# A planner's prices for TensorE, for whole float32 products and for the port that two engines share, in a two-layer encoder

## The chip, the core and the metric

The kernel runs on one core of one Trainium2 chip. The core has a matrix engine (TensorE, PE in the profile, with a second row PEld for its weight loads), VectorE (DVE), ScalarE (ACT), GpSimd (POOL), and SyncE (SP), which only issues transfers. The metric is the device time of one execution in microseconds; less is better.

## What is computed

The reference is a two-layer streaming encoder over 1024 tokens of 1024 values, in float32. Layer 0 mixes with a gated causal convolution of 31 taps beside a gated linear recurrence, layer 1 with differential attention (two softmax maps per head, eight heads, rotary positions, a mask by chunks of 64). After each mixer and each feed-forward part comes a residual sum and a layer norm:

```python
for layer in range(DEPTH):
    y = conv_lru_mixer(x, ...) if layer % 2 == 0 else diff_attention_mixer(x, ...)
    x = layer_norm(DN_ALPHA * x + y, mix_ln_g[layer], mix_ln_b[layer])
    x = layer_norm(DN_ALPHA * x + (silu(x @ w_gate) * (x @ w_up)) @ w_down, ffn_ln_g[layer], ffn_ln_b[layer])
```

The feed-forward part is 2816 wide.

## The kernel before

**Products.** A float32 product of full accuracy is made of three products in the engine's faster float32 format (fp32r): `three` takes operands that are split into a high part and a rest and issues high by high, high by rest, rest by high. `split` makes the two parts: ScalarE casts the source to the high part, and VectorE subtracts it from the source. This subtraction is the row `xt<-g,xt` or `g<-g,g ... fp32r` of the profile; when its source is in the matrix engine's result memory (PSUM, tile `PS`), it is `xt<-PS,xt`. Nearly all products are 128x128 by 512 columns. Four products alone, those of the mean and the variance in `conv_mean` and `conv_var`, are whole float32 ones of 512 columns; the profile shows each of them as two records `PS<-g,SM`. Transposes go through the matrix engine as well, with float32 operands (`PS<-SM,g 128x128`).

**Stages.** Layer 0's mixer runs first. Its second token half is mixed with the lead of the feed-forward part: `ffn_lead` computes two of the seven products of a Strassen-like scheme for each of the 22 strips of the hidden width, and `operands_b` turns tokens into operands by `x_operand`, which subtracts or adds on VectorE, transposes four blocks on PE and splits the result. `ffn_up` then takes one strip after another, with five products (60 matrix instructions) a strip: GpSimd adds or subtracts weight halves (`w_operand`), ScalarE casts, VectorE subtracts, PE multiplies, VectorE and GpSimd combine. `ffn_down` does seven more products. Layer 1 mixes attention with another stream twice: the first half of the queries with the projections of the later heads, the second half with the lead of the second feed-forward part. In attention, `attn_rms` has two GpSimd powers of one element for every pair of query blocks, 32 pairs in all, and each of the 32 layer norms has one.

**The planner.** Nothing of the order on an engine is left to the text of the program. Each instruction that is emitted is recorded by `Order.note`, with its dependences, a price in nanoseconds from `Order.price` and its engine. `Order.solve` then makes a schedule. Going backward it gives each instruction a due time: the matrix instructions are put in program order one behind the other by their prices, and what feeds them is due before them by its own price and by `lag`; on the other engines the due times are also pushed apart by 0.81 of the price. Going forward it plays the five engines in time: among what is ready, each engine takes the instruction due first, and its price is added to the engine's clock. At the end `apply` fixes the order found on every engine by dependences that cost no semaphore. The planned times go nowhere else: the chip runs the fixed orders at its own pace. The prices of instructions on VectorE, ScalarE and GpSimd, the constants `margin`, `press`, `tail`, `patience` and `switch`, and the emission with its own constant `MM` for mixing two streams are not touched by the change.

Of the kernel before, what the change touches and what calls it, by code (L numbers as in the profile page):

```python
# [10 lines left out]
F32 = mybir.dt.float32  # L11
# [73 lines left out]
class Order:  # L85
# [82 lines left out]
    def note(self, eng, name, ins, a, k):  # L168
        i = len(self.ops)
        deps = {}  # L170
        aps = [x for x in (*a, *k.values()) if hasattr(x, "ap") and hasattr(x, "tensor")]
        out = a[0] if a else k["out"]
        outs = [out] + [k[x] for x in ("accum_out",) if x in k]
        reads = [x for x in aps if not any(x is o for o in outs)]
        for x in reads:
            self.touch(i, deps, x, False)
        for x in outs:
            self.touch(i, deps, x, True)
        op = Op(i, ins, eng, deps)
        op.cost, op.table = self.price(eng, name, out, reads, a, k)  # L180
        op.dma = name == "dma_start"
        op.label = name
        self.ops.append(op)

    def price(self, eng, name, out, reads, a, k):
        n = 1
        for s in out.shape[1:]:
            n *= s
        if name == "dma_start":
            b = 4 * n * out.shape[0]  # L190
            return b / 360.0, None
        if eng == "pe":
            whole = reads[0].dtype == F32
            if name == "transpose":
                return 109.2, None
            if n < 256:
                return (214.0 if whole else 107.0), None
            return (n / 2.4 + 2.5) * (4 if whole else 1), None
        psum = any(x.name.startswith("PS") for x in (out, *reads))
        if eng == "act":  # L200
            f = a[2] if name == "activation" else None
            fn = str(f).split(".")[-1] if f is not None else "Copy"
            src = reads[0] if reads else out
            t = 0.833 * n + (52 if src.name.startswith("PS") else 94)
            if hasattr(k.get("bias"), "ap"):
                t += 50
            if hasattr(k.get("scale"), "ap"):
                t += 93 if not hasattr(k.get("bias"), "ap") else 137
            if "accum_out" in k:
                t += 93  # L210
            return t, SETS.get(fn)
        if eng == "dve":
            if name in ("tensor_reduce", "bn_stats"):
                n = 1
                for s in reads[0].shape[1:]:
                    n *= s
            if name in ("tensor_copy", "memset"):
                return (0.52 if name == "tensor_copy" and not psum else 1.0417) * n + (69 if name == "tensor_copy" else 7), None
            if name == "reciprocal":
                return 6.25 * n + 69, None  # L220
            t = 1.0417 * n + 69
            if name == "tensor_scalar":
                t = 0.75 * n + 70
            elif name == "scalar_tensor_tensor" and hasattr(a[2], "ap"):
                t += 61
            return t, None
        if eng == "pool":
            if n <= 4:
                return 1000.0 if name == "tensor_tensor" else 700.0, None
            return (2.7 * n + 150 if name == "tensor_tensor" else 0.9 * n + 280 if name == "tensor_scalar" else n + 60), None  # L230
        return 50.0, None
# [10 lines left out]
    def solve(self):  # L242
        ops = self.ops
        n = len(ops)
        succ = [[] for _ in range(n)]
        for o in ops:
            for d, raw in o.deps.items():
                succ[d].append((o.i, raw))

        t = 0.0  # L250
        late = [0.0] * n
        for o in ops:
            if o.eng == "pe":
                late[o.i] = t
                t += o.cost
        last = t
        gone = dict.fromkeys(self.ENGINES, 1e12)
        need = [len(x) for x in succ]
        heap = [(-1e12, -o.i) for o in ops if not need[o.i]]
        heapq.heapify(heap)  # L260
        while heap:
            i = -heapq.heappop(heap)[1]
            o = ops[i]
            dur = o.cost + (1100 if o.dma else 0)
            x = min((late[s] - self.lag(o, ops[s], raw) for s, raw in succ[i]), default=last + self.tail) - dur
            if o.eng == "pe":
                x = min(x, late[i])
            elif o.eng != "sp" and not o.dma:
                e = o.eng
                x = min(x, gone[e] - o.cost * self.press)  # L270
                gone[e] = x
            late[i] = x
            for d in o.deps:
                need[d] -= 1
                if not need[d]:
                    heapq.heappush(heap, (-min(late[s] - self.lag(ops[d], ops[s], raw) for s, raw in succ[d]), -d))
        self.late = late

        est = [0.0] * n
        left = [len(o.deps) for o in ops]  # L280
        free = dict.fromkeys(self.ENGINES, 0.0)
        ready = {e: [] for e in self.ENGINES}
        order = {e: [] for e in self.ENGINES}
        for o in ops:
            if not left[o.i]:
                ready[o.eng].append(o.i)
        table = None
        hw = ring = 0.0
        pick = {}
        dirty = set(self.ENGINES)  # L290
        self.start = [0.0] * n
        done = 0
        while done < n:
            for e in dirty:
                r = ready[e]
                if not r:
                    pick[e] = None
                    continue
                t0 = max(free[e], min(est[i] for i in r))
                slack = {"dve": 130, "act": 60, "pool": 60}.get(e, 0)  # L300
                best = None
                for i in r:
                    if est[i] > t0 + slack:
                        continue
                    key = late[i]
                    if est[i] > t0:
                        key += self.patience
                    if e == "act" and ops[i].table and table not in ops[i].table:
                        key += self.switch
                    if best is None or key < best[0]:  # L310
                        best = (key, i)
                pick[e] = (max(t0, est[best[1]]), best[1])
            dirty = set()
            e = min((p for p in pick if pick[p]), key=lambda p: pick[p][0])
            s, i = pick[e]
            o = ops[i]
            ready[e].remove(i)
            order[e].append(i)
            if e == "act" and o.table and table not in o.table:
                table = o.table[0]  # L320
                s += 1283
            self.start[i] = s
            if o.dma:
                if e == "pool":
                    free[e] = s + 900
                    b = free[e] + 2000
                else:
                    free[e] = s + 60
                    hw = max(hw, s + 25) + 450
                    b = hw + 1600  # L330
                ring = max(ring, b) + o.cost
                end = ring
            else:
                end = free[e] = s + o.cost
            dirty.add(e)
            for j, raw in succ[i]:
                est[j] = max(est[j], end + self.lag(o, ops[j], raw))
                left[j] -= 1
                if not left[j]:
                    ready[ops[j].eng].append(j)  # L340
                    dirty.add(ops[j].eng)
            done += 1
        self.total = max(free.values())
        return order
# [18 lines left out]


class Op:
    __slots__ = ("i", "ins", "eng", "deps", "cost", "table", "dma", "label")

    def __init__(self, i, ins, eng, deps):
        self.i, self.ins, self.eng, self.deps = i, ins, eng, deps
# [1588 lines left out]
```

## Time and profile before

| | us |
|---|---|
| median of 3 runs | 2277.43 |
| fastest and slowest run | 2267.81, 2277.70 |
| the profiled execution | 2272.42 |
| its span, first to last instruction | 2270.6 |
| PE busy in the span | 2151.8 (95%) |
| VectorE busy | 1852.9 (82%) |
| ScalarE busy | 1025.0 (45%) |
| GpSimd busy | 980.8 (43%) |

The profile is one execution. Busy time is that of instructions in flight; matrix instructions overlap, so what one of them takes from the engine is read from the distance between starts or from a count in a stretch, not from its own length. The engine's granted clock is a share of its full 2.4 GHz; the mean over the span is 0.979.

### The profile page before, as it was taken

To read this page: it belongs to the slowest core of one execution; us is meant where nothing else is said; L and a number is where in the kernel's file an instruction comes from. 1 tells how busy PE (TensorE), PEld (TensorE's weight loads), DVE (VectorE), ACT (ScalarE), POOL (GpSimd) and SP (SyncE) were. 2 spreads that over 40 slices of the span, in tenths; PEclk is the share of its full clock that TensorE was granted. 3 is DMA by queue.
4 is the path that set the end of the run, shared out by engine and by line. 5 is a ranking of instruction groups with operands and counts; after the bars stand their busy time and mean duration, and the time that the engine had idled before them with its cause. 6 is when DMAs were issued, how large, how long until landed. Compare 5 with 4: busy or idle time off the path is not lost.

```text
span 2270.6 us, 28995 instructions
## 1 busy us (share of the span) xinstructions
PE 2151.8 (95%) x9856; PEld 1769.1 (78%) x9856; DVE 1852.9 (82%) x2747; ACT 1025.0 (45%) x1791; POOL 980.8 (43%) x762
## 2 busy tenths in 40 slices
PE   9999898999999999989999997989989999999997
PEld 7877776778888888868878775877777888888885
DVE  8978799897888698884888867777878887778887
ACT  6485437343333334642455444555634333344362
POOL 1122412177777454221344324222334867755622
PEclk9999999999999999999999998999999999999999
DMA  8446986374454959846556589676737444477776
GB/s 238 94 111 158 264 240 192 116 271 150 149 159 153 317 142 224 224 112 208 160 160 176 150 238 245 187 192 173 199 107 254 167 160 158 161 210 249 177 181 170
DMA packets 173539, 419.74 MB, mean 185 GB/s; under 512 B 18896, under 2 KB 39120, under 8 KB 173392
## 3 DMA queue, kind: packets, MB, share of 16 engines
q1 hardware_dynamic: 145168, 364.47, 50.3%
q0 software_dynamic: 28224, 53.43, 13.9%
q8 instruction: 78, 1.28, 0.2%
q14 instruction: 69, 0.57, 0.1%
HBM read 313.03 MB, written 85.98 MB: 176 GB/s over the span
## 4 chain that ended last, share of the span: by engine, by line
PE 66%; DMA 16%; DVE 9%; issue 4%; ACT 3%; POOL 1%; SPq 1%; DVEq 0%; POOLq 0%; ACTq 0%
PE PS L380 66%; DVE g L380 6%; DMA g<-in_down 5%; DMA g<-in_up 4%; ACT g L380 2%; DMA g<-g 2%; DVE xt L380 2%; DMA z_d<-g 1%; DMA g<-k_d 1%; DVE SM L380 1%; POOL g L380 1%; DMA g<-a_d 1%; DMA g<-in_wout 1%; SPq L380 1%; DMA k_d<-g 1%
## 5 line engine op out<-in xcount | busy, mean ns | idle before, releaser
L380 POOL TENSOR_TENSOR g<-g,g 128x512 f32<-128x512 f32 (+1 forms) x368 | 601.1, 1645 | 518.2 <-DVE g L380 243.9
L380 PE MATMUL PS<-xt 128*128 128x512 f32 x2536 | 668.9, 392 | 15.3 <-ACT xt L380 6.6
L380 PE MATMUL PS<-g,xt 128*128 128x512 f32 (+1 forms) x2800 | 648.8, 379 | 11.9 <-ACT g L380 7.5
L380 PE MATMUL PS<-xt,g 128*128 128x512 f32 x2428 | 612.6, 401 | 37.6 <-ACT g L380 23.5
L380 PEld LDWEIGHTS PS<-g,xt 128*128 128x128 f32 x2800 | 516.2, 190 | 118.4 <-ACT g L380 11.1
L380 PEld LDWEIGHTS PS<-xt,g 128*128 128x128 f32 x2428 | 459.7, 192 | 143.2 <-ACT g L380 28.6
L380 PEld LDWEIGHTS PS<-xt 128*128 128x128 f32 x2536 | 475.9, 189 | 117.0 <-ACT xt L380 8.4
L380 ACT CAST xt<-g 128x512 fp32r<-128x512 f32 x567 | 334.5, 619 | 513.0 <-PE PS L380 330.8
L380 DVE TENSOR_TENSOR xt<-g,xt 128x512 fp32r<-128x512 f32 x567 | 496.9, 901 | 83.0 <-ACT xt L380 78.1
L380 DVE TENSOR_TENSOR g<-g,g 128x512 f32<-128x512 f32 (+2 forms) x442 | 449.5, 1027 | 68.8 <-ACT g L380 57.6
L380 DVE TENSOR_TENSOR g<-PS,g 128x512 f32<-128x512 f32 (+3 forms) x408 | 255.7, 641 | 131.8 <-PE PS L380 102.2
L380 ACT CAST g<-g 128x512 fp32r<-128x512 f32 (+1 forms) x212 | 167.2, 796 | 200.1 <-DVE g L380 67.2
L380 DVE SCALAR_TENSOR_TENSOR g<-g,SM,g 128x512 f32<-128x512 f32 (+20 forms) x301 | 250.2, 865 | 5.9 <-POOL SM L380 3.8
L380 ACT ACTIVATE g<-PS,SM 128x512 f32<-128x512 f32 (+8 forms) x266 | 179.4, 688 | 151.9 <-PE PS L380 91.8
L380 PE MATMUL PS<-xt,xt 128*128 128x512 f32 (+1 forms) x612 | 212.9, 390 | 0.0
L380 PE MATMUL PS<-g,g 128*128 128x512 f32 (+3 forms) x768 | 197.2, 367 | 13.8 <-ACT g L380 7.8
L380 PEld LDWEIGHTS PS<-g,g 128*128 128x128 f32 x768 | 132.6, 190 | 40.0 <-ACT g L380 10.3
L380 POOL DMA_DIRECT2D g<-in_down x88 | 84.4, 1053 | 169.8 <-DMA g<-in_down 161.4
L380 POOL TENSOR_TENSOR SM<-SM 128x1 f32<-128x1 f32 x96 | 85.0, 928 | 149.0 <-DVE SM L380 148.6
L380 POOL DMA_DIRECT2D g<-g x64 | 60.1, 1023 | 192.7 <-ACT g L380 131.8
L380 POOL TENSOR_TENSOR g<-g 128x512 f32<-128x512 f32 x74 | 114.0, 1581 | 63.1 <-DMA g<-in_gate 33.0
L380 PE MATMUL PS<-SM,g 128*128 128x128 f32 (+1 forms) x704 | 111.4, 284 | 29.8 <-DVE g L380 20.4
(49 smaller groups left out, 1200.4 us busy)
## 6 DMA issues: line engine op xcount, KB each, us to landing
g<-in_up SPq DMA_DIRECT2D x88, 512.0 KB, 4.3
g<-in_down SPq DMA_DIRECT2D x176, 256.0 KB, 3.6
z_d<-g SPq DMA_DIRECT2D x44, 512.0 KB, 4.5
g<-in_gate SPq DMA_DIRECT2D x44, 512.0 KB, 4.2
g<-z_d SPq DMA_DIRECT2D x44, 512.0 KB, 4.2
g<-in_down POOLq DMA_DIRECT2D x88, 256.0 KB, 6.7
a_d<-g SPq DMA_DIRECT2D x36, 512.0 KB, 2.9
g<-a_d SPq DMA_DIRECT2D x36, 512.0 KB, 6.7
```

Source lines behind the costliest of these rows:

```text
L380: r = f(*a, **k)
```

## The change

Only the planner's prices change; no instruction, buffer, or dependence of the computation is added or removed.

- A matrix instruction of at least 256 columns is priced at n/2.4 + 13.5 ns instead of n/2.4 + 2.5; with whole float32 operands at 2.9 n instead of four times the former price. Below 256 columns and for transposes the prices stay.
- In the forward play, the first matrix instruction that is not whole behind a transpose or a whole float32 one costs 88 ns more.
- Instructions with two tensors on VectorE and GpSimd, without an operand in PSUM and priced at over 300 ns, are marked as `pair`. When such an instruction starts on VectorE while one is under way on GpSimd, it goes on at 0.4 of its pace until GpSimd's has ended.

```diff
+        op.whole = eng == "pe" and (name == "transpose" or reads[0].dtype == F32)
+        op.pair = name in ("tensor_tensor", "scalar_tensor_tensor", "tensor_mul", "tensor_add", "tensor_sub") \
+            and len(reads) > 1 and not any(x.name.startswith("PS") for x in (out, *reads)) and op.cost > 300
...
-            return (n / 2.4 + 2.5) * (4 if whole else 1), None
+            return 2.9 * n if whole else n / 2.4 + 13.5, None
...
+        whole = False
+        slow = 0.4
+        shared = 0.0
...
-                end = free[e] = s + o.cost
+                cost = o.cost
+                if e == "pe":
+
+                    if whole and not o.whole:
+                        cost += 88
+                    whole = o.whole
+                elif e == "dve" and o.pair and s < shared:
+
+                    cost = cost / slow if cost < (shared - s) * slow else cost + (shared - s) * (1 - slow)
+                end = free[e] = s + cost
+                if e == "pool" and o.pair:
+                    shared = end
```

## Rows read from the trace of the kernel before

**Rows 1.** Busy time of the engines by stretch, with instruction counts, granted clock and transfers.

```profile
core 0: us, PE busy (x) PEld busy (x) DVE busy (x) ACT busy (x) POOL busy (x), PEclk, DMA share, GB/s
...
114.00:456.00 342.00, 310.73 (x1329) 248.26 (x1328) 297.56 (x433) 181.16 (x268) 85.38 (x82) 0.96 0.67 180
...
513.00:798.00 285.00, 285.00 (x1258) 235.77 (x1257) 215.56 (x249) 102.85 (x172) 188.62 (x123) 1.00 0.58 186
...
1083.00:1368.00 285.00, 273.97 (x1367) 227.76 (x1366) 234.45 (x467) 137.88 (x300) 110.07 (x91) 1.00 0.61 176
1368.00:1425.00 57.00, 41.91 (x181) 33.72 (x180) 43.34 (x68) 27.16 (x48) 21.94 (x15) 0.79 0.99 250
1425.00:1767.00 342.00, 312.03 (x1649) 261.00 (x1649) 270.48 (x456) 174.84 (x343) 115.35 (x108) 0.97 0.65 184
1767.00:2223.00 456.00, 455.31 (x2006) 375.99 (x2006) 371.52 (x456) 185.66 (x316) 281.75 (x196) 1.00 0.63 184
2223.00:2270.60 47.60, 33.77 (x136) 25.60 (x134) 33.76 (x53) 8.09 (x14) 10.27 (x9) 0.89 0.59 166
sum 2270.60, PE 2151.78 PEld 1769.11 DVE 1852.88 ACT 1025.02 POOL 980.78; mean PE 179.31 PEld 147.43 DVE 154.41 ACT 85.42 POOL 81.73
```

**Rows 2.** Waits of PE over the span: us in total, times, longest.

```profile
PE PS L380 <- ACT g L380: 45.3, 28, 5.4
PE PS L380 <- DVE g L380: 33.3, 27, 5.1
PE PS L380 <- DVE xt L380: 11.9, 5, 6.2
PE PS L380 <- ACT xt L380: 6.6, 5, 2.7
```

**Rows 3.** Timeline of PE, transposes in turn with products: start, length, count.

```profile
441.95 1.03 PE L380 MATMUL PS<-SM,g 128*128 128x128 f32 x8
442.74 3.02 PE L380 MATMUL PS<-xt,g 128*128 128x512 f32 x12
445.60 1.03 PE L380 MATMUL PS<-SM,g 128*128 128x128 f32 x8
```

**Rows 4.** Timeline of PE around one whole float32 product.

```profile
369.91 1.02 PE L380 MATMUL PS<-g,SM 128*128 128x512 f32 x2
370.37 5.35 PE L380 MATMUL PS<-xt,g 128*128 128x512 f32 x21
375.56 2.88 PE L380 MATMUL PS<-g,xt 128*128 128x512 f32 x12
```

**Rows 5.** Groups of instructions by shape, 513 to 798 us: busy, mean ns, idle before.

```profile
L380 POOL TENSOR_TENSOR g<-g,g 128x512 f32<-128x512 f32 x96 | 157.5, 1654 | 57.0 <-DVE g L380 49.2 <-DMA g<-a_d 4.8 <-DVE xt L380 2.8
...
L380 DVE TENSOR_TENSOR xt<-g,xt 128x512 fp32r<-128x512 f32 x115 | 106.9, 937 | 19.8 <-ACT xt L380 19.7
...
L380 DVE TENSOR_TENSOR g<-g,g 128x512 f32<-128x512 f32 x39 | 59.5, 1527 | 0.2
```

**Rows 6.** Groups of VectorE by shape, 114 to 456 us.

```profile
L380 DVE TENSOR_TENSOR g<-g,g 128x512 f32<-128x512 f32 x38 | 28.2, 766 | 0.7 <-DMA g<-g 0.6
```

**Rows 7.** Timeline of VectorE in one strip of `ffn_up`.

```profile
606.41 1.78 DVE L380 TENSOR_TENSOR g<-g,g 128x512 f32<-128x512 f32 x1
608.12 0.68 DVE L380 TENSOR_TENSOR g<-PS,g 128x512 f32<-128x512 f32 x1
608.72 1.18 DVE L380 TENSOR_TENSOR xt<-g,xt 128x512 fp32r<-128x512 f32 x1
```

**Rows 8.** Timeline of GpSimd in the same strip.

```profile
605.90 5.15 POOL L380 TENSOR_TENSOR g<-g,g 128x512 f32<-128x512 f32 x3
```

**Rows 9.** Timeline of VectorE beside a power of GpSimd.

```profile
1691.18 1.28 DVE L380 SCALAR_TENSOR_TENSOR g<-g,SM,g 128x1024 f32<-128x1024 f32 x1
```

**Rows 10.** Timeline of GpSimd at the same time.

```profile
1691.17 1.68 POOL L380 TENSOR_TENSOR SM<-SM 128x1 f32<-128x1 f32 x2
```

**Rows 11.** Groups over the span, GpSimd's powers.

```profile
L380 POOL TENSOR_TENSOR SM<-SM 128x1 f32<-128x1 f32 x96 | 85.0, 928 | 149.0 <-DVE SM L380 148.6
```

More of the change, by code (lines that the diff above doesn't have):

```diff
@@ L365 @@
 class Op:
-    __slots__ = ("i", "ins", "eng", "deps", "cost", "table", "dma", "label")
+    __slots__ = ("i", "ins", "eng", "deps", "cost", "table", "dma", "label", "whole", "pair")
     def __init__(self, i, ins, eng, deps):
```

## Prediction, made before the changed kernel had run

> **What bounds the kernel now.** I read the table of stretches first, because the average over the span (PE busy 2151.8 of 2270.6 us) says little about a kernel of many stages [rows 1]. The reader is to see two kinds of stretch. In 513 to 798 us, most of the first `ffn_up`, PE is busy for all 285.00 us, at full clock, and does 1258 matrix instructions of 512 columns: 285.00 / 1258 = 0.2266 us each. The stretch 1767 to 2223 is like it, with 0.7 us idle in 456. There PE is the bound and no order of the instructions can bring anything. The other kind is where two streams are mixed or a stage turns into the next. From 114 to 456 PE is idle 342.0 - 310.7 = 31.3 us and from 1425 to 1767 342.0 - 312.0 = 30.0 us. Attention's first half, 1083 to 1368, has 11.0, the turn between the halves 15.1, and the end of the kernel 13.8 [rows 1]. All idle time is 2270.6 - 2151.8 = 118.8 us.
>
> Where PE idles its granted clock falls: 0.96, 0.79 and 0.97 in those stretches against 1.00 in the dense ones [rows 1]. In the two long mixed stretches the missing share is 0.04 x 342 + 0.03 x 342 = 24 us beside 61.3 us of idleness, so one microsecond of idleness takes about 0.39 us more with it.
>
> The waits of PE come next. ScalarE's and VectorE's results end 45.3 + 33.3 + 11.9 + 6.6 = 97.1 us of it in 65 waits, none longer than 6.2 us [rows 2]. The longest wait for ScalarE, 5.4 us, is the start of the kernel. So about 92 us are waits for something that stood in a queue of an engine, and these an order can shorten or lengthen. That is the ground on which the change can act.
>
> **The change part by part.** Nothing is removed or added on the chip. Every gain or loss comes from other orders, so for each price I ask two things: does it come nearer to the rows, and does it act where PE waits?
>
> *PE's step.* 512 columns were priced at 512/2.4 + 2.5 = 215.8 ns and are now priced at 226.8. The row is 226.6 [rows 1]. Before, the planner ran PE 4.8% too fast. In a stretch of 342 us its PE was some 16 us ahead of the chip's, while VectorE's unshared two-tensor instruction, priced at 1.0417 x 512 + 69 = 602 ns, is right: 608.12 to 608.72 is 0.60 us from start to start [rows 7]. So in the mixed stretches the old plan saw VectorE as nearer to being the bound than it is. Where a result seemed late to it, it drew another stream's products forward, and PE then came to the drawn ones first. The new price takes this error away over the whole kernel. It acts in both kinds of stretch, and it is worth nothing in the dense ones.
>
> *88 ns behind a transpose.* Eight transposes and twelve products take 445.60 - 441.95 = 3.65 us [rows 3]. The old prices make 8 x 0.1092 + 12 x 0.2158 = 3.46, the new ones 0.874 + 2.722 + 0.088 = 3.68. With the measured step and no surcharge it would be 3.59, so the row shows some 0.06 us of the 0.088. The new sum is off by 0.03 instead of by 0.19; nearly all of the betterment is the step's.
>
> *Whole float32 products.* Their price goes from 863 to 2.9 x 512 = 1485 ns. From 369.91 to 375.56 is 5.65 us, with 21 products of 0.2266 = 4.76 in it, which leaves 0.89 us for the whole one [rows 4]. The old price was the better one here. There are four such products, so at most 4 x 0.62 = 2.5 us of plan: I take nothing, and between 0 and 2.5 us lost.
>
> *The shared port.* In `ffn_up` the subtractions of `split` take 937 ns on average and the two-tensor ones of results 1527, and GpSimd is busy 188.6 of 285 us [rows 1, 5]. By the new rule a start under GpSimd finds on average half of 1654 ns left and loses 0.6 of it, 0.5 us, in 0.66 of the cases: 602 + 0.33 us = 930 ns. That is close to the 937. But this is the stretch without idle PE, and VectorE has 69 us of its 285 to spare there. In the mixed stretch 114 to 456 GpSimd is busy 85 us of 342, and the same kind of instruction takes 766 ns [rows 1, 6], of which some 0.08 us are overlap with its neighbour (0.68 long, 0.60 from start to start [rows 7]). Hence the largest correction falls where nothing is to be won: I take 0, between 0 and what a spoiled strip costs (below).
>
> One row speaks against the form of this price. GpSimd's three instructions from 605.90 last 5.15 us, so they end near 607.6, 609.3 and 611.0 [rows 8]. VectorE's instruction that starts at 606.41 ends at 608.19, and that of 608.72 at 609.90: each is 0.6 us behind GpSimd's end, as if it had stood still until then [rows 7]. So the planner counts 0.6 of a wait that is whole, and is still short by up to 0.4 of 1.65 us. The Trainium skill says the same ("SBUF — State Buffer", section "Who interferes with whom"): a two-input VectorE instruction and a GpSimd one that reads SBUF exclude each other for a whole instruction, and the later one blocks. By that rule and the trace agreeing with it, a plan made with 0.4 of the pace can still bring a result too late. That is rival D.
>
> *Powers counted as users of the port.* GpSimd's `tensor_tensor` of one element is priced at 1000 ns and has two tensors, so it is marked too. A VectorE instruction of 1024 columns beside two powers takes 1.28 us, no more than its price of 1.20 and the overlap [rows 9, 10]. The planner will add up to 0.6 us to VectorE for each of the 96 powers [rows 11] that does not exist. That is rival C.
>
> *The sum.* I take a sixth of the idleness of the two long mixed stretches as saved, 61.3 / 6 = 10 us, by the right step. The sixth is a choice between nothing and a half. It is nearer to nothing because the error was 5% of a step and many waits are bursts that no order avoids. With the clock's 0.39 it is 14 us: 2272.4 - 14 = 2258.5 us for the profiled execution's own time. That execution lies 5.0 us under the median of the three runs, so the median goes from 2277.4 to 2263 us, 0.6% less. The runs shown differ by 9.9 us, 0.4%, so I take 0.5% as what can be told from no change.
>
> **The rivals.**
>
> *B, no change that can be told.* A hundred choices between ready instructions come out otherwise, some better, some worse. For it: waits are many and short, 65 with a mean of 1.5 us [rows 2], and constants such as the 0.81 and the 70 ns margin stay as they were beside the old step. Against it: the step's error was the same everywhere. Time: 2277, within 11 us.
>
> *C, slower by the powers.* Of the 96 powers 64 are in attention, two for each of 32 pairs. In the plan each holds VectorE's next two-tensor instruction by up to 0.6 us, 38 us in all; what waits for it is planned later, and products of the other stream are put ahead of it in PE's order. On the chip the result is there early and stands. Attention's chain is then longer than its companion stream, and PE waits at the end of the mix. If half of it comes to that, 19 us x 1.39 = 27: 2304 us. It decides from about 8 us of idleness, a fifth, where it has eaten up more than my gain. For it: VectorE is busy 234 of 285 and 270 of 342 us there [rows 1]. Against it: PE has spare work from the other stream for most of the time, and idles only 11 us in the first half.
>
> *D, a strip loses its cover.* If in each of the 44 strips of `ffn_up` one result on PE's path comes 0.4 x 0.85 = 0.34 us later than planned, the dense stretches lose 15 us: 2292. For it the three rows above; against it the 69 us of spare VectorE time.
>
> *E, much faster.* The right step halves the 92 us of waits: 46 x 1.39 = 64, so 2213. For it speaks only that nearly all waits are for queues; against it that the turn of the halves has the transfers busy at 0.99 [rows 1].
>
> **How the numbers follow.** Forecast A (a little faster) 0.38, B 0.26, C 0.19, D 0.09, E 0.08. Faster by over 0.5% are A and E, 0.46; slower C and D, 0.28; the same B, 0.26. The time is A's, 2263 us, with its own range 2248 to 2266. The range over the cases reaches into E, to half its way (2230), and past C's 2304 to 2308; it leaves out 0.07 below and 0.09 above.
>
> **What would show it.** Right step: the dense stretches again at 0.2266 us an instruction with no idleness, and idleness of PE in 114 to 456 and 1425 to 1767 under 55 us together, with the clock there at 0.97 or more. B: other waits with a like sum. C: waits of PE on VectorE or ScalarE growing in the two halves of attention. D: idle PE in 513 to 798. The prediction is wrong if the mixed stretches lose more than they had, or if transfers on SyncE's queue, which is ordered anew as well, come later at the turns between stages.

## The result, and the profile after

The changed kernel takes 2292.52 us (median of 4 runs, 2291.0 to 2295.4) beside 2276.1 us for the kernel before (also the median of 4 runs): a ratio of 1.0091 with a 95% interval of 1.0070 to 1.0112. It is slower by 0.9%, where 0.6% faster was forecast; the time itself lies in the range.

The profiled execution has a span of 2289.1 us, 18.5 more than before. PE is busy 2160.4 of it, so it idles 128.7 us, 9.9 more. The other 8.6 us are busy time, with the same instructions. The mean granted clock over the span is 0.975 after 0.979, and 0.025 x 2289.1 - 0.021 x 2270.6 = 9.5 us, which is these 8.6 within the rounding of the clock. So idleness and clock share the loss about evenly in these two executions. One execution does not fix the clock's part: the 25 runs of the kernel before that stand beside e1 have clocks of 0.974 to 0.982 and times of 2263 to 2285 us.

To find the place, I cut both executions where PE has done the same number of instructions. First the kernel before, busy time of the engines by stretch (columns as in [rows 1]):

```profile
121.60:262.60 141.00, 126.05 (x532) 101.02 (x531) 112.67 (x156) 88.23 (x119) 41.32 (x41) 0.94 0.65 169
262.60:459.40 196.80, 180.48 (x782) 143.75 (x781) 181.43 (x274) 89.21 (x147) 43.01 (x40) 0.97 0.68 194
459.40:790.80 331.40, 329.13 (x1451) 271.14 (x1450) 265.87 (x304) 124.19 (x210) 228.58 (x148) 1.00 0.60 196
790.80:1097.50 306.70, 296.77 (x1332) 244.93 (x1330) 241.85 (x342) 127.84 (x220) 108.95 (x91) 0.98 0.67 184
1097.50:1303.60 206.10, 199.33 (x1001) 166.70 (x1000) 177.72 (x352) 100.26 (x220) 86.80 (x68) 1.00 0.56 161
1303.60:1405.70 102.10, 85.14 (x401) 68.52 (x400) 73.63 (x138) 48.42 (x93) 40.61 (x33) 0.92 0.87 235
1405.70:1749.60 343.90, 312.22 (x1653) 261.57 (x1652) 268.18 (x461) 175.97 (x346) 102.05 (x101) 0.96 0.66 186
1749.60:2204.60 455.00, 454.31 (x2001) 375.15 (x2000) 373.09 (x448) 182.06 (x312) 284.36 (x193) 1.00 0.62 186
```

Then the changed kernel, the same counts of PE's instructions:

```profile
121.80:264.00 142.20, 122.55 (x532) 98.12 (x532) 122.14 (x161) 84.02 (x116) 44.10 (x43) 0.94 0.68 178
264.00:469.70 205.70, 185.27 (x781) 146.09 (x780) 180.29 (x271) 88.72 (x145) 36.93 (x37) 0.94 0.62 178
469.70:800.10 330.40, 328.81 (x1451) 271.27 (x1450) 266.32 (x304) 124.30 (x210) 228.84 (x149) 1.00 0.60 196
800.10:1108.20 308.10, 298.52 (x1332) 245.03 (x1331) 239.97 (x344) 129.12 (x221) 110.38 (x90) 0.98 0.66 184
1108.20:1321.50 213.30, 202.56 (x1002) 168.95 (x1001) 180.52 (x357) 100.63 (x221) 89.77 (x70) 0.99 0.55 160
1321.50:1414.80 93.30, 83.80 (x401) 68.93 (x400) 73.82 (x127) 46.06 (x90) 37.77 (x30) 0.92 0.82 237
1414.80:1766.80 352.00, 314.58 (x1652) 259.80 (x1651) 269.88 (x463) 178.83 (x349) 105.10 (x102) 0.96 0.65 183
1766.80:2221.20 454.40, 454.07 (x2001) 375.10 (x2000) 381.98 (x452) 182.57 (x312) 285.29 (x194) 1.00 0.62 188
```

Line against line the length changes by +1.2, +8.9, -1.0, +1.4, +7.2, -8.8, +8.1 and -0.6 us; the start and the end of the kernel, outside the table, add 0.2 and 1.9. The dense stretches (third and last) keep their time. The mixed ones lose: layer 0's second one 8.9, attention's first half 7.2, its second half 8.1. The turn between the halves gains 8.8. In the second line four of the nine microseconds are idle time (20.4 after 16.3 us), and the clock is 0.94 after 0.97.

The stretch that answers to the dense row of [rows 1] is the same to the digit:

```profile
513.00:798.00 285.00, 285.00 (x1258) 235.82 (x1257) 222.64 (x258) 105.08 (x176) 189.67 (x123) 1.00 0.57 184
```

The waits of PE in the changed kernel, which answer to [rows 2]:

```profile
PE PS L397 <- ACT g L397: 47.0, 29, 6.4
PE PS L397 <- DVE g L397: 32.9, 28, 4.2
PE PS L397 <- DVE xt L397: 15.5, 7, 7.1
PE PS L397 <- DMA g<-k_d: 7.2, 4, 2.8
PE PS L397 <- ACT xt L397: 6.1, 5, 2.7
```

These are other waits with nearly the same sum: the first, second, third and fifth row, for ScalarE and VectorE, make 101.5 us in 69 waits, after 97.1 in 65.

In attention's first half PE waits longer for the transfers of `k_d`, which SyncE issues and whose order is new as well. Before (1083 to 1306 us), and after (1083 to 1326):

```profile
PE PS L380 <- DMA g<-k_d: 1.5, 2, 0.8
PE PS L397 <- DMA g<-k_d: 6.0, 3, 2.8
```

That is 4.5 us more, about what PE's idle time grows by in that stretch (10.7 after 6.8). At the turn between the halves PE's waits for transfers shrink (2.9 after 6.5 us), and over the span they make 8.9 after 8.0.

The longest wait of all can be followed. PE, the rows around it:

```profile
242.08 2.35 PE L397 MATMUL PS<-SM,g 128*128 128x128 f32 x20
244.65 0.66 PE L397 MATMUL PS<-SM,g 128*128 128x128 f32 x4 [0.22 <-DVE g L397]
249.26 1.12 PE L397 MATMUL PS<-SM,g 128*128 128x128 f32 x4 [3.96 <-ACT g L397]
257.48 0.76 PE L397 MATMUL PS<-xt,g 128*128 128x512 f32 x1 [7.10 <-DVE xt L397]
```

VectorE at that time; the last row is the first of the five instructions from 248.02, by itself:

```profile
245.70 0.74 DVE L397 SCALAR_TENSOR_TENSOR g<-g,SM,g 128x512 f32<-128x512 f32 x1
...
248.02 8.71 DVE L397 SCALAR_TENSOR_TENSOR g<-g,SM,g 128x512 f32<-128x512 f32 x5
256.65 0.68 DVE L397 TENSOR_TENSOR xt<-PS,xt 128x512 fp32r<-128x512 f32 x1
...
248.02 6.06 DVE L397 SCALAR_TENSOR_TENSOR g<-g,SM,g 128x512 f32<-128x512 f32 x1
```

And GpSimd:

```profile
248.19 2.38 POOL L397 TENSOR_SCALAR g<-g 128x1024 f32<-128x1024 f32 x2
...
250.81 2.73 POOL L397 TENSOR_SCALAR g<-g 128x1024 f32<-128x1024 f32 x2
```

PE has run 28 transposes and stands until VectorE's `xt<-PS,xt` has split one of their results. That one is queued behind five convolution taps that take 8.71 us, although one alone takes 0.74. Nearly all of it is the first tap: 6.06 us, from 248.02 to 254.08. The other four need 2.65 us together. Meanwhile GpSimd scales the residual rows (`residual`) in four one-input instructions, the last of which ends at 253.54; the tap ends 0.54 us behind it. The planner prices the five taps at 5 x 0.66 = 3.3 us, before and after the change, since only two-tensor instructions of GpSimd are marked as users of the port. So one of the changed kernel's new waits comes from a conflict that the new price leaves out. It is an example and no account of the loss: this stretch is only 1.2 us longer in all, and e13 below, which loses 0.2%, has the same kind of wait, 6.81 us, behind a first tap of 5.31.

### The profile page after: what moved, and what is told of

Same layout as the page of the kernel before. It is cut to its first block, busy times and chain, and to the rows that moved or that the text cites. A ratio compares the mean times of both kernels' runs of the same rounds, so it can differ in the third digit from the quotient of the medians.

```text
span 2289.1 us, 29008 instructions
## 1 busy us (share of the span) xinstructions
PE 2160.4 (94%) x9856; PEld 1771.0 (77%) x9856; DVE 1872.4 (82%) x2747; ACT 1022.6 (45%) x1788; POOL 981.1 (43%) x762
## 4 chain that ended last, share of the span: by engine, by line
PE 45%; DMA 9%; DVE 6%; issue 2%; ACT 1%; POOL 1%; SPq 0%; POOLq 0%; DVEq 0%; ACTq 0%
PE PS L397 45%; DMA g<-in_down 4%; DVE g L397 3%; DMA g<-in_up 2%; DVE SM L397 2%; DMA g<-k_d 1%; ACT g L397 1%; DMA g<-a_d 1%; POOL g L397 1%; SPq L397 0%; DVE xt L397 0%; POOL SM L397 0%; DMA x_d<-g 0%; DMA z_d<-g 0%; DMA xt<-k_d 0%
## 5 line engine op out<-in xcount | busy, mean ns | idle before, releaser
L397 PE MATMUL PS<-g,xt 128*128 128x512 f32 (+3 forms) x2800 | 643.3, 378 | 10.3 <-DVE g L397 6.4
L397 DVE TENSOR_TENSOR xt<-g,xt 128x512 fp32r<-128x512 f32 x567 | 509.6, 924 | 69.6 <-ACT xt L397 59.3
L397 DVE SCALAR_TENSOR_TENSOR g<-g,SM,g 128x512 f32<-128x512 f32 (+16 forms) x301 | 256.2, 886 | 5.7 <-POOL SM L397 3.6
L397 PE MATMUL PS<-xt,xt 128*128 128x512 f32 x612 | 213.0, 390 | 0.4 <-ACT xt L397 0.4
L397 POOL DMA_DIRECT2D g<-in_down x88 | 78.2, 944 | 174.7 <-DMA g<-in_down 161.2
```

Of the source, the lines that this page charges most:

```text
L397: r = f(*a, **k)
```

## The experiments

Theory S was that the right step itself makes the worse order; theory C that the powers do (rival C); theory L that any new order of this planner is a draw, and the old one stood at the fast end. All ratios are against runs of the kernel before on the same chip, with 95% intervals. "Old" kernels are the kernel before with one edit; "changed" ones are the changed kernel with one edit.

**Parts of the change alone**

e1, old, with the step alone:

```diff
-            return (n / 2.4 + 2.5) * (4 if whole else 1), None
+            return (n / 2.4 + 2.5) * 4 if whole else n / 2.4 + 13.5, None
```

> Only the price of a fast product changes (512 columns: 226.8 instead of 215.8 ns); no surcharge, no port, old price of whole products. Theory S (the right step itself makes the worse order): at least two thirds of the 18.5 us are here, 2287 to 2297 us. Theory C (the port rule with the powers does it): no change or a gain, 2262 to 2279. Theory L (every new order loses against a lucky old one): 2282 to 2297, as for any other price.

Measured: 2299.22 us, 1.0116 (1.0068 to 1.0163). The step alone costs as much as the whole change. Theory C's number is missed by 20 us; those of S and L, up to 2297, are overshot by 2.

e2, old, with the lines of the port rule, powers included:

```diff
+                elif e == "dve" and o.pair and s < shared:
+                    cost = cost / slow if cost < (shared - s) * slow else cost + (shared - s) * (1 - slow)
...
+                if e == "pool" and o.pair:
+                    shared = end
```

> Only the port rule, the powers included. Theory C: 2285 to 2300 us, with the loss in attention's first half. Theory S: 2270 to 2282. Theory L: 2282 to 2297.

Measured: 2277.3 us, 1.0026 (0.9998 to 1.0054): not told from no change, as theory S had it. Theory C falls as the cause, and theory L's number is missed too.

e3, old, with the surcharge alone:

```diff
+                    if whole and not o.whole:
+                        cost += 88
+                    whole = o.whole
```

> Only the 88 ns behind a transpose or a whole product. It moves 205 of 6805 places on the matrix engine. Theories S and C: 2270 to 2282 us. Theory L: 2280 to 2297.

Measured: 2276.38 us, 1.0014 (0.9992 to 1.0035). As S and C had it: no loss that can be told. Theory L's 2280 is missed.

e6, old, with half of the step:

```diff
+            return (n / 2.4 + 2.5) * 4 if whole else n / 2.4 + 8.0, None
```

> Half of the step's correction alone (221.3 ns). Theory S: half of the 25.7 us of the full step, 2280 to 2290 us. Theory L: anywhere in 2278 to 2300, with no rule in it.

Measured: 2286.36 us, 1.0049 (1.0025 to 1.0072). It fits both theories.

e7, old, the 11 ns of the step (`o.more`) added only in the forward play:

```diff
+                    cost += o.more
```

> The right step only in the forward play, where the engines' clocks are kept; due times by the old price. 400 places move on the matrix engine. Theory S in the play: 2290 to 2300 us. Theory S in the due times: 2270 to 2280. Theory L: 2280 to 2300 here and in the next one.

Measured: 2306.95 us, 1.0134 (1.0100 to 1.0167).

e8, old, the 11 ns added only in the due times:

```diff
-                t += o.cost
+                t += o.cost + o.more
...
-            dur = o.cost + (1100 if o.dma else 0)
+            dur = o.cost + o.more + (1100 if o.dma else 0)
```

> The right step only in the due times, the play with the old price. 877 places move on the matrix engine. Theory S in the due times: 2290 to 2300 us. Theory S in the play: 2270 to 2280. Theory L: 2280 to 2300.

Measured: 2287.89 us, 1.0055 (1.0034 to 1.0076). Both halves of the step lose, and 1.3 and 0.6% don't add up to the 1.2 of both. Theory S in either form wanted one of the two without a loss. Theory L's span, up to 2300, holds for e8 and is overshot by e7.

**Controls at the old step**

e4 and e5, old, 1 ns more and 1 ns less:

```diff
+            return (n / 2.4 + 2.5) * 4 if whole else n / 2.4 + 3.5, None
```

```diff
+            return (n / 2.4 + 2.5) * 4 if whole else n / 2.4 + 1.5, None
```

> Control: the old prices with 1 ns more for a fast product (216.8 instead of 215.8), which corrects a tenth of the error and moves 478 of 6805 places on the matrix engine. Theory S: 2274 to 2280 us, a tenth of the loss at most. Theory L: 2282 to 2297, about as much as the whole change.

> Control on the other side: the old prices with 1 ns less for a fast product (214.8 ns), further from the measured step; 371 of 6805 places move. Theory S (the right step makes the worse order, in proportion): 2270 to 2275 us, no loss. Theory L (any new order loses against a lucky old one): 2280 to 2295, as the nudge upward did.

Measured: 2287.09 us, 1.0063 (1.0039 to 1.0087), and 2285.2 us, 1.0056 (1.0033 to 1.0079). This is the main reading. A price that is half a per cent higher, or lower, loses about two thirds of what the change loses. In proportion, S would allow 0.1% up and a gain down. Theory L's numbers hold in both.

e11 and e12, old, half a nanosecond more and less:

```diff
+            return (n / 2.4 + 2.5) * 4 if whole else n / 2.4 + 3.0, None
```

```diff
+            return (n / 2.4 + 2.5) * 4 if whole else n / 2.4 + 2.0, None
```

> The old prices with half a nanosecond more for a fast product; 491 of 6805 places move on the matrix engine. Theory L: 2278 to 2295 us, as with a whole nanosecond. If a smaller nudge cost less: 2272 to 2278.

> The old prices with half a nanosecond less; 243 places move. Theory L: 2278 to 2295 us. If a smaller nudge cost less: 2272 to 2278.

Measured: 2280.25 us, 1.0028 (1.0007 to 1.0048), and 2275.77 us, 1.0008 (0.9990 to 1.0026). By their medians the smaller nudges lost less. e11 is inside theory L's span; e12, which moves the fewest places of the four, lost nothing that can be told. So theory L is too strong where it says that every new order loses as much. How many places move is no measure of it either: e3 and e12, with 205 and 243, lost nothing that can be told, but e11 with 491 lost less than e5 with 371, and e7 with 400 lost most of all.

e18, old, with another constant, nothing of the step:

```diff
-    press = 0.81
+    press = 0.80
```

> The old prices, and the constant that pushes the due times of the other engines apart at 0.80 instead of 0.81; nothing of the step is touched, and 493 of 6805 places move on the matrix engine. Theory L (any new order loses against the old one, whatever made it): 2280 to 2295 us. If only the step's price matters: 2268 to 2278.

Measured: 2279.52 us, 1.0034 (1.0012 to 1.0056). The time lies a little under theory L's span and over that of the rival, but the ratio is a loss clear of no change. A redrawn order loses without any touch to the step.

**Draws at the right step**

e9, e10, e13, e14, e15 and e17, changed, with the fast product at 225.8, 227.8, 225.3, 226.3, 227.3 and 224.3 ns:

```diff
-            return 2.9 * n if whole else n / 2.4 + 13.5, None
+            return 2.9 * n if whole else n / 2.4 + 12.5, None
```

The others have 14.5, 12.0, 13.0, 14.0 and 11.0 in the same place.

> The whole change with the fast product at 225.8 instead of 226.8 ns. Theory L (the old order was a lucky draw, every new one is worse by about as much): 2280 to 2300 us, the mean of this and the next near the 0.6% of the two nudges of the old price. Theory S (on top of that, the right step itself costs): both at 0.9% and more, 2290 to 2305.

> The whole change with the fast product at 227.8 ns. The same as for the one before: theory L 2280 to 2300 us, theory S 2290 to 2305.

> The whole change with the fast product at 225.3 ns, 0.9 ns from what one chip record shows. Theory L (a lottery of orders): anywhere in 2270 to 2300 us, without order among the neighbours. Theory S (the right step costs by itself): above 2285, and on average with the other draws at the right step clearly over the mean of the nudges of the old step, 0.4%.

> The whole change with the fast product at 226.3 ns. The same: theory L 2270 to 2300 us, theory S above 2285.

> The whole change with the fast product at 227.3 ns. The same: theory L 2270 to 2300 us, theory S above 2285.

> The whole change with the fast product at 224.3 ns, one nanosecond on in the direction in which the losses fell (1.2, 0.8, 0.9, 0.5, 0.2, 0.2% from 227.8 down to 225.3). If a trend of the step is behind that order (theory S in a milder form: the step should be under the measured one): 2265 to 2278 us, no loss or a gain. Theory L (neighbours are draws): anywhere in 2270 to 2300.

Measured, in order of the price, the changed kernel among them:

| priced step, ns | run | median, us | ratio, interval |
|---|---|---|---|
| 224.3 | e17 | 2278.37 | 1.0035 (1.0016 to 1.0053) |
| 225.3 | e13 | 2279.69 | 1.0016 (1.0002 to 1.0031) |
| 225.8 | e9 | 2276.44 | 1.0024 (1.0001 to 1.0048) |
| 226.3 | e14 | 2284.49 | 1.0046 (1.0030 to 1.0062) |
| 226.8 | changed | 2292.52 | 1.0091 (1.0070 to 1.0112) |
| 227.3 | e15 | 2291.98 | 1.0077 (1.0050 to 1.0104) |
| 227.8 | e10 | 2299.56 | 1.0121 (1.0089 to 1.0153) |

Against the expectations, e9 lies under both spans, e13 and e14 lie under theory S's 2285, and e10 and e15 fit both theories. Prices that are all within about 1% of the measured 226.6 [rows 1] give losses from 0.2 to 1.2%. Their mean is 0.59%, that of the five old kernels with a small nudge (e4, e5, e11, e12, e18) 0.38%. Both sets scatter by more than the 0.2 between them, so theory S as an addition to L is neither shown nor excluded. The fall from 227.8 down to 225.3 looked like a trend. e17 did not go on with it: it lost 0.35%, where the trend wanted no loss, and its time is 0.4 us over the trend's span. It is inside theory L's span, which is too wide to be much of a test.

The seven are not seven independent draws. Place by place in the traces, with matrix instructions told apart by names and shape alone, the changed kernel's sequence differs from the old one at 1198 of 9856 places, but from those of e14, e15 and e10 at only 213, 125 and 274.

Where the draws differ is seen in e10 by stretches of the same counts as above (attention's second half and the dense end):

```profile
1406.50:1773.00 366.50, 318.13 (x1653) 261.97 (x1651) 272.99 (x467) 178.67 (x350) 104.63 (x102) 0.95 0.63 176
1773.00:2231.90 458.90, 455.84 (x2002) 376.32 (x2001) 383.51 (x453) 182.12 (x312) 283.26 (x194) 1.00 0.62 186
```

and in e13 for the same two and layer 0's mixed ones:

```profile
122.60:260.10 137.50, 121.80 (x531) 97.82 (x530) 121.83 (x162) 84.25 (x116) 42.86 (x42) 0.96 0.69 184
260.10:460.90 200.80, 180.33 (x781) 142.79 (x780) 178.99 (x269) 88.34 (x145) 37.77 (x38) 0.97 0.64 181
...
1406.10:1756.50 350.40, 314.15 (x1651) 258.72 (x1650) 270.94 (x465) 179.41 (x350) 105.58 (x104) 0.97 0.66 186
1756.50:2212.30 455.80, 454.43 (x2001) 375.04 (x2000) 382.88 (x455) 182.62 (x312) 285.46 (x194) 1.00 0.62 187
```

Prices 2.5 ns apart make 366.5 and 350.4 us of the same 1650 instructions, while PE is busy 318 and 314. The idle time makes most of the difference: 48 us against 36.

**The powers**

e16, changed, with the powers of one element no longer marked:

```diff
-            and len(reads) > 1 and not any(x.name.startswith("PS") for x in (out, *reads)) and op.cost > 300
+            and len(reads) > 1 and not any(x.name.startswith("PS") for x in (out, *reads)) and op.cost > 300 and out.shape[-1] > 4
```

> The whole change, but GpSimd's powers of one element are no longer counted as users of the port; 161 places move on the matrix engine against the changed kernel. Theory C (the powers make attention wait): back to 2265 to 2278 us, with the gain in attention. Theory L: 2275 to 2300 with no rule in it.

Measured: 2288.11 us, 1.0055 (1.0038 to 1.0072). It stays slow, inside theory L's span and 10 us over theory C's; the 0.36% under the changed kernel is no more than half a nanosecond of step gives (e14). Theory C is not borne out.

## Why the prediction was wrong

*The bound, and where time can move.* Right. The dense stretches kept 285.00 us and 454.4 after 455.0; all that moved, moved in the mixed stretches and the turns. The prediction's mark for a right forecast, idleness under 55 us in the two long mixed stretches, was missed: in the matched stretches idleness there is 19.7 + 20.4 + 37.4 = 77.5 us, after 63.0. The clock there, 0.94, 0.94 and 0.96, missed its 0.97 as well.

*The prices one by one.* The readings stand: the dense row of the changed kernel gives the 226.6 ns of the step again. It also has no idle PE, so rival D did not come about. Rival C's mark came in part: in attention's second half PE's waits for VectorE and ScalarE grew from 31.5 to 36.9 us. But the powers are not their cause, by e2 and e16. VectorE is busy 19.5 us longer with the same instructions, 1872.4 after 1852.9. This does not order the losses: e9 has 1871.3 and loses 0.2%, e7 has 1858.1 and loses 1.3%.

*The sum.* This is the step that failed: "I take a sixth of the idleness of the two long mixed stretches as saved, 61.3 / 6 = 10 us, by the right step". It held that a truer price makes a better order. Instead of 10 us less, idleness in the mixed stretches became 14.5 us more, 77.5 after 63.0. The step alone lost 1.2% (e1). Seven kernels whose step is within about 1% of the measured one lost 0.2 to 1.2%, and none gained.

*Rival B.* It had the mechanism and the wrong centre. It said that many choices come out otherwise, some better, some worse, and put the outcome around no change. The 19 kernels with a new order, the changed one included, have ratios from 1.0008 to 1.0134, with a mean of 1.0055; 16 of the intervals lie wholly above 1 and none below. So shown is that the old order stands at the fast end of those that nearby prices give, and that a new order loses without any correction of the step (e5, e18). Why it stands there is not shown: constants chosen by measured times with the old prices would do it, but no run tells; and three of the others (e2, e3, e12) can't be told from it.

*The size.* A new order near the old price costs 0.4% on average, less than half of what the change lost. The five kernels with the whole step at 226.8 ns or more (e1, e10, e15, e16 and the changed one) lose 0.92% on average, the five at 221.3 to 226.3 (e6, e9, e13, e14, e17) only 0.34. This grouping was made after the runs, and the kernels from 226.3 up have orders much closer to each other than to the old one. Whether the rest comes from the step itself or from what these orders share is open.

*The clock.* The factor of 1.39 for idleness was too small here: 9.9 us of idleness came with 8.6 us of longer busy time. One factor does not carry over between executions: in e13 PE idles 125.4 us at a mean clock of 0.982, in e6 122.6 at 0.972. What else sets the clock is not shown.

*Left open.* Whether the right step costs something of its own; and what marking GpSimd's one-input instructions as users of the port would do, which was not tried.

## What to carry to other kernels

A fixed order from a planner is one draw: before a changed price is credited or blamed, run a few kernels whose price is off by a hair, and compare the changed one with their spread and not with the old kernel alone. Count how much of the order such neighbours share before taking them for independent draws. A truer price did not shorten the waits here. And read the idle stretches first: the largest correction here, the shared port in `ffn_up`, fell where the matrix engine never waits.

## What the runs showed of the hardware

GpSimd's one-input `TENSOR_SCALAR` of 1024 columns held up a VectorE instruction that reads two tensors. The tap of 6.06 us, 0.74 when alone, ended 0.54 us behind the last of four of them; beside two-input ones the distance was 0.6 us [rows 7, 8]. There VectorE got through behind one GpSimd instruction; here one tap stood through all four, and in e13 one of 5.31 us did the same. GpSimd's powers of one element did not lengthen a VectorE instruction beside them [rows 9, 10].
